# One plain half of the up projection instead of two: product 2 summed in PSUM onto a copy of product 1, and the rows of hn made on two engines

## The chip, the cores and the metric

The kernel runs on one core of one Trainium2 chip. The metric is the device time of one execution in microseconds (us); lower is better.

## What is computed

One encoder layer on 512 tokens of width 2048, all in float32. The change lies in the second half of the layer:

```python
h = rms_norm(x, pre_ffn_g)                        # 512 x 2048
up = causal_dwconv(h @ w_up, conv_w, conv_b)      # w_up is 2048 x 11264
y = (gelu(up[..., :5632]) * up[..., 5632:]) @ w_down
x = x + rms_norm(y, post_ffn_g)
```

`causal_dwconv` is a three-tap convolution along the tokens, channel by channel. Ahead of it stand the attention, the pooling and the projection with `w_o`, which the change does not touch.

## The kernel before

**Numbers.** Every matmul operand is split into a rounded high part (ScalarE, line 140) and a low rest (VectorE, line 141). A plain product is three matmuls of 512 columns: high by high, high by low, low by high (`mm3`, lines 162, 164 and 165).

**Units and halves.** The up projection is cut into 22 units `u` with two halves each: `p = 0` goes through the gelu (`gate`), `p = 1` is multiplied onto it (`product`). A half is 256 channels. Channels lie on the partitions and the 512 tokens along the free axis.

**Two ways to compute a half.** The first `PLAIN` halves are plain: 16 blocks of 128 rows of the contraction, by 2 blocks of channels, by 3 matmuls, 96 matmuls in all. Every other half `k` uses seven products of 2 by 2 blocks in place of eight (channel blocks, halves of the contraction, halves of the tokens), numbered 1 to 7. One product (`mm2`) is 8 wide matmuls (line 170: the high part of the weight factor by the high and low parts of the token factor side by side, 512 columns) and 8 narrow ones (line 176: the low part of the weight factor by the high part of the token factor, 256 columns). Products in `TURNED` (4, 6 and 7) issue the narrow ones first.

**Factors.** The token factors are made once. `turn_back` transposes the normalized rows `hn` on TensorE (line 1012), ScalarE scales them out of PSUM (line 1017) into whole blocks, and they are split into `hT` (printed as `gT`), which serve products 1, 2, 4 and 7. `h_sums` then forms the sums for products 5, 6 and 3 on VectorE (lines 1381 to 1387) and splits them (tiles `h5`, `h6`, `h3`); it also turns the block for product 7 into a difference, which is split back into `hT`. The weight factors are made on the fly. `Factors.load` brings a block of `w_up` from HBM, `make` splits it into `wfh` and `wfl`, and then an adding DMA of GpSimd (`add`, line 1110) puts another block on top of the raw tile, which makes the next factor that shares it. For product 7 of a half the tile is the one of product 3 (`wy`): split for 3, then added to, then split for 7. There are four pairs of `wfh` and `wfl`.

**Banks.** Products 1, 6, 7 and 4 of a half accumulate in one PSUM bank `qa`; ScalarE copies the sum out after 6 and after 7 (lines 1421 and 1427). Products 5 and 3 use `qg` (3 uses `qe` in the first four halves), product 2 uses `qd`. After product 1, ScalarE copies one half of `qa` and VectorE adds the other half (lines 1406 and 1407); after product 2, VectorE adds both halves of `qd` (lines 1410 and 1411).

**Order.** The order of the products on TensorE is a table (`Factors.order`): first products 1 and 2 of halves 0 to 3, while `hn` is still being made for tokens 256 to 511; then the plain halves, between which the transposes are placed by hand; then products 5, 3, 6, 7 and 4 of the halves 0 to 3; then all seven products of each later half, interleaved with the half before, at places 7 apart. TensorE runs in the order in which the code is written. On the other engines a scheduler fixes the order when the program is built. Each of these engines works through its queue in that order. `sums_in_dram` (`more_sums`) issues copies and adding DMAs of 1 MB blocks of `w_down` beside this; one step is issued after each quarter of a plain half.

Of the kernel before, what the change touches and what calls it, by code (L numbers as in the profile page):

```python
# [15 lines left out]
P = 128  # L16
# [11 lines left out]
EPS = 1e-6  # L28
WARM = 9
NU = KF // 2  # L30
PLAIN = 2
CU = 4
AHEAD = 3
SCALE = 1.0 / math.sqrt(DH)
# [47 lines left out]
def encoder_layer(ctx: ExitStack, tc: tile.TileContext, x, xT, vecs, rel, post_mix, post_ffn,  # L82
# [23 lines left out]
    def bank(name):  # L106
        return psum.tile([P, 512], F32, tag="ps", name=name)
# [107 lines left out]
    def part(w, *idx):  # L215
        return tuple(v[(slice(None),) + idx] for v in w)
# [685 lines left out]
    if True:  # L902
# [100 lines left out]
        def quarter(k, t, i):  # L1003

            return tuple(hT[2 * k + i][:, :, at, :] for at in AT[t])

        def turn_back(t0, pair, ps):

            for k in range(2):
                kb = 2 * pair + k  # L1010
                for t in range(2):
                    nc.tensor.transpose(ps[:, k * T + t * P:k * T + (t + 1) * P],
                                        hn[t0 + t][:, kb * P:(kb + 1) * P], ident)
            v = wholes[pair // 4, t0 // 2]
            for k in range(2):
                kb = 2 * pair + k
                nc.scalar.activation(v[:, kb % 8, :], ps[:, k * T:(k + 1) * T], AF.Copy, scale=col(V_PREFFN, kb))
            if pair % 2:
                i = pair // 2 % 2
                split(*quarter(pair // 4, t0 // 2, i), v[:, 4 * i:4 * i + 4, :])  # L1020
# [43 lines left out]
        class Factors:  # L1064
# [3 lines left out]
            def __init__(self):  # L1068
                n = 2 * NU - PLAIN

                self.alone, self.open = (1, 2, 3, n - 1), False
                place_of = {1: 0, 6: 8, 2: 2, 7: 10, 5: 4, 4: 12, 3: 6}
                begin = [(k, i) for k in range(4) for i in (1, 2)]
                lone = {5: 0, 3: 2, 6: 4, 7: 6, 4: 8}
                end = [(n - 1, 5), (n - 2, 6), (n - 1, 3), (n - 1, 1), (n - 2, 7), (n - 1, 6), (n - 2, 4),
                       (n - 1, 7), (n - 1, 2), (n - 1, 4)]
                order = sorted([(5 * k + at, k, i) for k in range(4) for i, at in lone.items()] +
                               [(18.5 + 7 * (k - 4) + at, k, i) for k in range(4, n) for i, at in place_of.items()])  # L1080
                self.order = begin + [(k, i) for _, k, i in order if (k, i) not in begin + end] + end
                self.order[8:8] = [("w", q) for q in range(4 * PLAIN)]
                self.raw, self.made, self.loaded, self.used = {}, [], 0, 0
# [75 lines left out]
            hn[t] = acc8(f"hn{t}", "A")  # L1159
        for l in range(2):  # L1160
            cs = slice(l * D // 2, (l + 1) * D // 2)
            for t in range(2, 4):
                nc.vector.tensor_scalar_mul(hn[t][:, cs], xn[t][:, cs], rn[:, t:t + 1])
        for k in range(2):
            wholes[k, 1] = whole_tile(h8(2 + k, f"a2{k + 1}"))

# [139 lines left out]
    if True:  # L1306
# [67 lines left out]
        def h_sums():  # L1374
            def keep(n, i, at, v):
                hs.setdefault(n, {})[i] = h8(at, f"h{n}{i}", F32R).rearrange("p (a b c) -> p a b c", a=4, b=2)
                split(*(hs[n][i][:, :, p, :] for p in range(2)), v)

            halves = [[wholes[k, t][:, 4 * i:4 * i + 4, :] for k in range(2) for t in range(2)] for i in range(2)]
            for i, (a11, a21, a12, a22) in enumerate(halves):  # L1380
                nc.vector.tensor_sub(a22, a22, a21)
                keep(5, i, (1, 0)[i], a22)
                nc.vector.tensor_sub(a21, a11, a21)
                nc.vector.scalar_tensor_tensor(a22, a22, -1.0, a11, op0=ALU.mult, op1=ALU.subtract)
                keep(6, i, (4, 5)[i], a22)
            for a11, a21, a12, a22 in halves:
                nc.vector.scalar_tensor_tensor(a12, a22, -1.0, a12, op0=ALU.mult, op1=ALU.subtract)
            for i in range(2):
                keep(3, i, (3, 2)[i], halves[i][2])
            return [v[1] for v in halves]  # L1390

        banks, gates = {}, {}

# [8 lines left out]
        def keep(k, i):  # L1402

            if i == 1:
                v = zs[k, "1"] = first_parts[:, k % 4, :]
                nc.scalar.activation(v, banks[k, "a"][:, :T], AF.Copy)
                nc.vector.tensor_add(v, banks[k, "a"][:, T:], v)
            elif i == 2:
                v, d = zs[k, "1"], banks.pop((k, "d"))
                nc.vector.tensor_add(v, d[:, :T], v)  # L1410
                nc.vector.tensor_add(v, d[:, T:], v)
            elif i in (5, 3) and k < 4:
                return
            elif i == 5:
                zs[k, "5"] = raw_x("zb")[:, :S] if k == end else holder("m8")[1]
                nc.scalar.activation(zs[k, "5"], banks[k, "g"], AF.Copy)  # L1416
            elif i == 6:
                m = raw_x("zm") if k == end else holder("m8")[2]
                zs[k, "m"] = m.rearrange("p (a b c) -> p a b c", a=2, b=2)
                v = wide(zs[k, "m"][:, :1])  # L1420
                keep.copied = nc.scalar.activation(v, banks[k, "a"], AF.Copy).ins
                nc.vector.tensor_add(v, banks[k, "g"] if k < 4 else banks.pop((k, "g")), v)
                if k < 4:
                    nc.vector.tensor_add(v, banks.pop((k, "e")), v)
            elif i == 7:
                v = wide(zs[k, "m"][:, 1:])
                nc.scalar.activation(v, banks[k, "a"], AF.Copy)
                nc.vector.tensor_add(v, banks.pop((k, "g")) if k < 4 else zs.pop((k, "5")), v)
            elif i == 4:
                keep_all(k)  # L1430

        def keep_all(k):
            one, m, a = zs.pop((k, "1")), zs.pop((k, "m")), banks.pop((k, "a"))
            z = new_z()
            nc.scalar.activation(z[:, 0, :T], one, AF.Copy)
            nc.vector.tensor_add(z[:, 1].rearrange("p (a b) -> p a b", a=2), m[:, :, 0], m[:, :, 1])
            nc.scalar.activation(z[:, 0, T:], a[:, T:], AF.Copy)
            nc.vector.tensor_add(z[:, 0, T:], a[:, :T], z[:, 0, T:])
            u, p = divmod(PLAIN + k, 2)
            if p:  # L1440
                product(u, gates.pop(u), z)
            elif k == 2:
                zs["late"] = u, z
            else:
                gates[u] = gate(u, z)

        def seven(k, i):
            w = factors.get()
            at = "e" if i == 3 and k < 4 else BANK[i]
            fresh = i in FIRST or at == "e"  # L1450
            if fresh:
                banks[k, at] = bank(f"q{at}_{k}")
            mm2(banks[k, at], w, [h_factor(i, kb) for kb in range(8)], fresh, i in TURNED)
# [25 lines left out]
        turn(2, 3)  # L1479
        behind_h.append((split.last, split.rest))  # L1480
        factors.open = True
        def plain(p, behind):
            ups = [bank(f"up{p}_{j}") for j in range(2)]
            for q in range(4):
                factors.used += 1
                factors.prefetch(0)
                with ExitStack() as behind_split:
                    for ins in behind_h[q] if not p and q < 2 else ():
                        behind_split.enter_context(tc.issue_after(ins))
                    factors.prefetch(factors.AHEAD if p else (1, 2, 3, factors.AHEAD)[q])  # L1490
                w = weights.get(f"w{p}0_{q}", 0)
                for kb in range(4 * q, 4 * q + 4):
                    for j in range(2):
                        mm3(ups[j], part(w, j, slice(kb % 4 * P, (kb % 4 + 1) * P)), g_both(hT, kb),
                            kb == 0, kb == KD - 1)
                behind(q)
            return ups

        def turn_two(q):
            if q < 2:  # L1500
                turn(4 + 2 * q, 5 + 2 * q)

        def keep_a21(q):
            more_sums(1)
            if q < 2:
                split(*quarter(0, 1, q), a21_11[q])

        ups = plain(0, turn_two)
        a21_11 = h_sums()
        gates[0] = gate(0, plain_z(ups))  # L1510
        ups = plain(1, keep_a21)
        product(0, gates.pop(0), plain_z(ups))
        rights, firsts = [right(0, cc) for cc in range(2)], []
        for r in rights:
            next(r)
# [6 lines left out]
        for k, i in factors.order[8 + 4 * PLAIN:]:  # L1522
            seven(k, i)
            keep(k, i)
            if (k, i) == (3, 6):
                u, z = zs.pop("late")
                with tc.issue_after(keep.copied):
                    gates[u] = gate(u, z)
# [260 lines left out]
```

## Time and profile before

| | |
|---|---|
| median of 3 runs | 1849.39 us (1848.6 to 1849.62) |
| profiled execution | 1850.36 us, of which the span of the trace is 1848.6 us |
| TensorE busy | 1838.0 us, 99% of the span |
| VectorE, ScalarE, GpSimd busy | 1483.9, 1099.8 and 306.6 us |
| the two plain halves and the transposes between them | 572.8 to 618.4 us |

The span is the time from the first to the last instruction of the trace. In a timeline row the first number is the start, the second the duration in us; rows that follow each other with the same form are merged and counted (x8). Square brackets give the idle time of the engine just before, and what ended it. PE is TensorE, PEld its weight loads, DVE VectorE, ACT ScalarE, POOL GpSimd, SP SyncE; SPq and POOLq are DMA queues.

### The profile page before, as it was taken

To read this page: it belongs to the slowest core of one execution; us is meant where nothing else is said; L and a number is where in the kernel's file an instruction comes from. 1 tells how busy PE (TensorE), PEld (TensorE's weight loads), DVE (VectorE), ACT (ScalarE), POOL (GpSimd) and SP (SyncE) were. 2 spreads that over 40 slices of the span, in tenths; PEclk is the share of its full clock that TensorE was granted. 3 is DMA by queue.
4 is the path that set the end of the run, shared out by engine and by line. 5 is a ranking of instruction groups with operands and counts; after the bars stand their busy time and mean duration, and the time that the engine had idled before them with its cause. 6 is when DMAs were issued, how large, how long until landed. Compare 5 with 4: busy or idle time off the path is not lost.

```text
span 1848.6 us, 25317 instructions
## 1 busy us (share of the span) xinstructions
PE 1838.0 (99%) x9514; PEld 1578.3 (85%) x9514; DVE 1483.9 (80%) x1776; ACT 1099.8 (59%) x1438; POOL 306.6 (17%) x407
## 2 busy tenths in 40 slices
PE   9999999999999999999999999999999999999998
PEld 7888888888888888888888888888888888888886
DVE  6988778878678787777777777777777899899876
ACT  7655555457586666665656666666655655555553
POOL 3411000100001222122122222221221011111101
PEclk9999999999999999999999999999999999999999
DMA  8599978999979988988889899898888977777785
GB/s 319 170 320 301 320 228 235 276 262 318 337 270 291 214 198 208 208 199 200 207 205 198 203 201 204 196 209 201 204 176 302 360 222 162 193 215 176 177 230 158
DMA packets 139546, 428.63 MB, mean 232 GB/s; under 512 B 12000, under 2 KB 15456, under 8 KB 133728
## 3 DMA queue, kind: packets, MB, share of 16 engines
q0 software_dynamic: 55440, 175.66, 47.0%
q1 hardware_dynamic: 83984, 251.36, 38.5%
q8 instruction: 75, 1.23, 0.3%
q14 instruction: 47, 0.39, 0.1%
HBM read 372.97 MB, written 104.33 MB: 258 GB/s over the span
## 4 chain that ended last, share of the span: by engine, by line
PE 98%; DMA 1%; DVE 0%; SPq 0%; issue 0%; ACT 0%; DVEq 0%; POOLq 0%; POOL 0%; ACTq 0%
PE qa L170 19%; PE qa L176 10%; PE qg L170 9%; PE qg L176 5%; PE qd L170 5%; PE pa L164 4%; PE pa L165 4%; PE pa L162 4%; PE m L165 3%; PE m L164 3%; PE m L162 3%; PE qd L176 2%; PE pg L164 2%; PE pg L165 2%; PE pg L162 2%; PE v L164 2%
## 5 line engine op out<-in xcount | busy, mean ns | idle before, releaser
L170 PE MATMUL qa<-gT,wfh 128*128 128x512 f32 x1176 | 294.4, 392 | 0.0
L141 DVE TENSOR_TENSOR wfl<-x,wfh 128x1024 fp32r<-128x1024 f32 x161 | 197.0, 1224 | 83.0 <-ACT wfh L140 80.8
L170 PEld LDWEIGHTS qa<-gT,wfh 128*128 128x128 f32 x1176 | 211.6, 189 | 37.9
L140 ACT ACTIVATE wfh<-x 128x1024 fp32r<-128x1024 f32 x161 | 170.1, 1057 | 92.4 <-PE qg L170 46.2
L1110 POOL DMA_DIRECT2D x<-in_w_up x122 | 104.6, 858 | 460.8 <-DVE wfl L141 429.2
L176 PE MATMUL qa<-gT,wfl 128*128 128x256 f32 x1176 | 164.5, 283 | 0.0
L170 PE MATMUL qg<-h,wfh 128*128 128x512 f32 x640 | 158.2, 389 | 0.6 <-ACT m L1416 0.6
L176 PEld LDWEIGHTS qa<-gT,wfl 128*128 128x128 f32 x1176 | 154.8, 191 | 4.1
L170 PEld LDWEIGHTS qg<-h,wfh 128*128 128x128 f32 x640 | 120.0, 188 | 25.9 <-ACT m L1416 1.0
L141 DVE TENSOR_TENSOR bl<-b,bh 128x2048 fp32r<-128x2048 f32 x56 | 127.1, 2286 | 18.4 <-ACT bh L140 11.7
L140 ACT ACTIVATE wfh<-wy 128x1024 fp32r<-128x1024 f32 x98 | 103.3, 1054 | 63.7 <-PE qd L170 49.6
L140 ACT ACTIVATE bh<-b 128x2048 fp32r<-128x2048 f32 x56 | 106.0, 1912 | 55.5 <-DVE b L1230 23.0
L141 DVE TENSOR_TENSOR wfl<-wy,wfh 128x1024 fp32r<-128x1024 f32 x98 | 119.4, 1218 | 10.2 <-ACT wfh L140 7.9
L162 PE MATMUL pa<-bh,ah 128*128 128x512 f32 x320 | 124.5, 389 | 0.0
L164 PE MATMUL pa<-bl,ah 128*128 128x512 f32 x320 | 124.5, 389 | 0.0
L165 PE MATMUL pa<-bh,al 128*128 128x512 f32 x320 | 124.5, 389 | 0.0
L170 PE MATMUL qd<-gT,wfh 128*128 128x512 f32 x392 | 97.0, 390 | 0.0
L176 PEld LDWEIGHTS qg<-h,wfl 128*128 128x128 f32 x640 | 87.3, 190 | 6.2
L176 PE MATMUL qg<-h,wfl 128*128 128x256 f32 x640 | 89.2, 282 | 0.0
L170 PEld LDWEIGHTS qd<-gT,wfh 128*128 128x128 f32 x392 | 73.3, 188 | 15.0
L170 PE MATMUL qa<-h,wfh 128*128 128x512 f32 x336 | 84.1, 392 | 0.0
L141 DVE TENSOR_TENSOR wfl<-wz,wfh 128x1024 fp32r<-128x1024 f32 x49 | 59.9, 1222 | 28.5 <-PE qa L170 25.4
(574 smaller groups left out, 4335.9 us busy)
## 6 DMA issues: line engine op xcount, KB each, us to landing
x<-in_w_up POOLq DMA_DIRECT2D x122, 512.0 KB, 6.5
b<-in_w_down SPq DMA_DIRECT2D x32, 1024.0 KB, 6.8
wt<-in_w_o POOLq DMA_DIRECT2D x24, 1024.0 KB, 15.5
wz<-in_w_up SPq DMA_DIRECT2D x42, 512.0 KB, 6.0
x<-in_w_up SPq DMA_DIRECT2D x42, 512.0 KB, 5.1
wy<-in_w_up SPq DMA_DIRECT2D x42, 512.0 KB, 4.2
wy<-in_w_up POOLq DMA_DIRECT2D x42, 512.0 KB, 6.6
sum<-part POOLq DMA_DIRECT2D x38, 512.0 KB, 6.9
```

Source lines behind the costliest of these rows:

```text
L140: rounded = nc.scalar.activation(hi, src, AF.Copy)
L141: rest = nc.vector.tensor_sub(lo, src, f32(hi))
L162: nc.tensor.matmul(ps, l[0], r[0], start=first, stop=False, skip_group_check=onto)
L164: nc.tensor.matmul(low, l[0], r[1], start=False, stop=False, skip_group_check=onto)
L165: nc.tensor.matmul(ps, l[1], r[0], start=False, stop=last, skip_group_check=onto)
L170: nc.tensor.matmul(ps, w[0][:, kb], pairs[kb][0], start=fresh and not kb, stop=last, skip_group_check=not fresh)
L176: nc.tensor.matmul(ps[:, sl], w[1][:, kb], pair[:, sl], start=False, stop=last, skip_group_check=not fresh)
L1110: nc.gpsimd.dma_start(self.raw[k, what], self.block(k, m, kh), accum_op=ALU.add)
```

## The change

There is now one plain half, and the half that was plain is computed in seven products, as half `k = 0` of 43 where there were 42. What else is written differently:

```diff
-PLAIN = 2
+PLAIN = 1
...
-                    nc.tensor.transpose(ps[:, k * T + t * P:k * T + (t + 1) * P],
-                                        hn[t0 + t][:, kb * P:(kb + 1) * P], ident)
+                    nc.tensor.matmul(ps[:, k * T + t * P:k * T + (t + 1) * P], hn[t0 + t][:, kb * P:(kb + 1) * P],
+                                     ident, start=not k and not t, stop=True, is_transpose=True,
+                                     skip_group_check=True)
...
-                begin = [(k, i) for k in range(4) for i in (1, 2)]
+                begin = [(0, 1), (1, 1), (0, 2), (2, 1), (1, 2), (3, 1), (2, 2), (3, 2)]
...
-                order = sorted([(5 * k + at, k, i) for k in range(4) for i, at in lone.items()] +
+                order = sorted([(1 if (k, i) == (1, 5) else 5 * k + at, k, i) for k in range(4) for i, at in lone.items()] +
...
-            for t in range(2, 4):
-                nc.vector.tensor_scalar_mul(hn[t][:, cs], xn[t][:, cs], rn[:, t:t + 1])
+            nc.scalar.activation(hn[2][:, cs], xn[2][:, cs], AF.Copy, scale=rn[:, 2:3])
+            nc.vector.tensor_scalar_mul(hn[3][:, cs], xn[3][:, cs], rn[:, 3:4])
...
             if i == 1:
-                v = zs[k, "1"] = first_parts[:, k % 4, :]
-                nc.scalar.activation(v, banks[k, "a"][:, :T], AF.Copy)
-                nc.vector.tensor_add(v, banks[k, "a"][:, T:], v)
+                banks[k, "d"] = bank(f"qd_{k}")
+                keep.copied = nc.scalar.activation(banks[k, "d"], banks[k, "a"], AF.Copy).ins
             elif i == 2:
-                v, d = zs[k, "1"], banks.pop((k, "d"))
-                nc.vector.tensor_add(v, d[:, :T], v)
+                v, d = first_parts[:, k % 4, :], banks.pop((k, "d"))
+                zs[k, "1"] = v
+                nc.scalar.activation(v, d[:, :T], AF.Copy)
                 nc.vector.tensor_add(v, d[:, T:], v)
...
-            fresh = i in FIRST or at == "e"
+            fresh = i in (1, 5) or at == "e"
...
-        ups = plain(0, turn_two)
-        a21_11 = h_sums()
+        turn(4, 5)
+        ups = [bank(f"up0_{j}") for j in range(2)]
+        for q in range(4):
...
+            more_sums(1)
+            if not q:
+                turn(6, 7)
+            if q == 1:
+                h_sums()
         gates[0] = gate(0, plain_z(ups))
-        ups = plain(1, keep_a21)
-        product(0, gates.pop(0), plain_z(ups))
...
-            if (k, i) == (3, 6):
+            if (k, i) in ((2, 7), (5, 1)):
```

So product 2 no longer starts its bank afresh: it adds onto a ScalarE copy of product 1 and waits for that copy. The transposes of pairs 4 and 5 stand ahead of the plain half instead of after its first quarter. `h_sums` is written after the second quarter of the only plain half instead of after the first of two; the split of the difference for product 7 is now inside it. Row block 2 of `hn` is made by ScalarE, row block 3 by VectorE.

On VectorE, this is the stretch that leads up to the low part of the weight factor of product 3 of half 0 (`wfl` from `wy`). In the kernel before:

```order
L141 TENSOR_TENSOR h61_5671<-a22_5257,h61_5671 128x4x256
L1311 SCALAR_TENSOR_TENSOR zc_5682<-zc_5682,vec_69 128x511 x2
L141 TENSOR_TENSOR h30_5676<-a12_5003,h30_5676 128x4x256
L1312 SCALAR_TENSOR_TENSOR zc_5682<-zc_5682,vec_69 128x510 x2
L141 TENSOR_TENSOR wfl_5695<-wx_5150,wfh_5694 128x1024
L141 TENSOR_TENSOR gT0_4822<-a21_5256,gT0_4822 128x4x256
L141 TENSOR_TENSOR wfl_5727<-wy_5537,wfh_5726 128x1024
```

In the changed kernel:

```order
L141 TENSOR_TENSOR h61_5597<-a22_5257,h61_5597 128x4x256
L141 TENSOR_TENSOR gT0_4822<-a21_5256,gT0_4822 128x4x256
L141 TENSOR_TENSOR gT1_4823<-a21_5256,gT1_4823 128x4x256
L141 TENSOR_TENSOR h30_5606<-a12_5003,h30_5606 128x4x256
L141 TENSOR_TENSOR wfl_5618<-x01_5497,wfh_5617 128x1024
L141 TENSOR_TENSOR h31_5609<-a12_5003,h31_5609 128x4x256
L141 TENSOR_TENSOR wfl_5650<-wy_5500,wfh_5649 128x1024
L141 TENSOR_TENSOR wfl_5655<-wx_5150,wfh_5654 128x1024
```

The low part of product 3's factor stands in both behind nearly all of `h_sums`; from the first row of `h_sums` (line 1382) to it there are 20 VectorE instructions in the changed kernel.

On ScalarE, this is the stretch that holds the high part of the factor of product 7 of half 0 and the copy of `qa` after product 6. In the kernel before (`wfh_5835` is the factor):

```order
L1310 ACTIVATE m8_5822<-zc_5682,vec_69 128x512
L140 ACTIVATE wfh_5835<-wy_5537 128x1024
L1435 ACTIVATE zc_5682<-first_parts_5274 128x256
L140 ACTIVATE wfh_5856<-wy_5622 128x1024
L1310 ACTIVATE m8_5822<-zc_5682,vec_69 128x512
L140 ACTIVATE wfh_5878<-wx_5150 128x1024
L1421 ACTIVATE m8_5822<-qa_0_5275 128x512
```

In the changed kernel (`wfh_5696` is the factor):

```order
L140 ACTIVATE wfh_5649<-wy_5500 128x1024
L140 ACTIVATE wfh_5654<-wx_5150 128x1024
L1437 ACTIVATE zc_5684<-first_parts_5274 128x256
L140 ACTIVATE wfh_5696<-wy_5500 128x1024
L1334 ACT_TABLE_LOAD
L1334 ACTIVATE zc_5684<-zc_5684 128x1024
L140 ACTIVATE wfh_5717<-wy_5547 128x1024
L1423 ACTIVATE m8_5784<-qa_0_5275 128x512
```

The table load and the gelu of unit 0 now stand between this factor and the copy of `qa`; in the kernel before they stand nine rows ahead of this factor.

More of the change, by code (lines that the diff above doesn't have):

```diff
@@ L1385, in h_sums @@
                 keep(6, i, (4, 5)[i], a22)
-            for a11, a21, a12, a22 in halves:
+            for i, (a11, a21, a12, a22) in enumerate(halves):
                 nc.vector.scalar_tensor_tensor(a12, a22, -1.0, a12, op0=ALU.mult, op1=ALU.subtract)
             for i in range(2):
+                split(*quarter(0, 1, i), halves[i][1])
+            for i in range(2):
                 keep(3, i, (3, 2)[i], halves[i][2])
-            return [v[1] for v in halves]
         banks, gates = {}, {}
@@ L1426, in keep @@
                 v = wide(zs[k, "m"][:, 1:])
-                nc.scalar.activation(v, banks[k, "a"], AF.Copy)
+                keep.copied = nc.scalar.activation(v, banks[k, "a"], AF.Copy).ins
                 nc.vector.tensor_add(v, banks.pop((k, "g")) if k < 4 else zs.pop((k, "5")), v)
@@ L1441, in keep_all @@
                 product(u, gates.pop(u), z)
-            elif k == 2:
+            elif k in (1, 3):
                 zs["late"] = u, z
@@ L1481, in encoder_layer @@
         factors.open = True
[L1482 to L1503, printed above, removed]
+        turn(4, 5)
+        ups = [bank(f"up0_{j}") for j in range(2)]
+        for q in range(4):
+            factors.used += 1
+            factors.prefetch(0)
+            with ExitStack() as behind_split:
+                for ins in behind_h[q] if q < 2 else ():
+                    behind_split.enter_context(tc.issue_after(ins))
+                factors.prefetch((1, 2, 3, factors.AHEAD)[q])
+            w = weights.get(f"w00_{q}", 0)
+            for kb in range(4 * q, 4 * q + 4):
+                for j in range(2):
+                    mm3(ups[j], part(w, j, slice(kb % 4 * P, (kb % 4 + 1) * P)), g_both(hT, kb),
+                        kb == 0, kb == KD - 1)
             more_sums(1)
-            if q < 2:
-                split(*quarter(0, 1, q), a21_11[q])
-        ups = plain(0, turn_two)
-        a21_11 = h_sums()
+            if not q:
+                turn(6, 7)
+            if q == 1:
+                h_sums()
         gates[0] = gate(0, plain_z(ups))
-        ups = plain(1, keep_a21)
-        product(0, gates.pop(0), plain_z(ups))
         rights, firsts = [right(0, cc) for cc in range(2)], []
```

## The prediction

> **What bounds the kernel now.** I read the page first: busy time by engine, and the chain that ended last.
>
> ```profile
> PE 1838.0 (99%) x9514; PEld 1578.3 (85%) x9514; DVE 1483.9 (80%) x1776; ACT 1099.8 (59%) x1438; POOL 306.6 (17%) x407
> PE 98%; DMA 1%; DVE 0%; SPq 0%; issue 0%; ACT 0%; DVEq 0%; POOLq 0%; POOL 0%; ACTq 0%
> ```
>
> TensorE is the chain. Then the waits of TensorE over the whole trace, of which this is the longest that is not at the program's start:
>
> ```profile
> PE qg L170 <- ACT m L1416: 0.6, 1, 0.6
> ```
>
> So only TensorE's own work can be saved, any new wait of TensorE costs its full length, and what VectorE saves is worth nothing by itself. Third, TensorE's timeline around the plain halves: start of the second plain half, start of the seven-product part (0,5), start of product (0,7), and a later product, ten products after (0,5).
>
> ```profile
> 596.57 0.39 PE L162 MATMUL up<-gT,w_0h 128*128 128x512 f32 x1
> ...
> 618.33 1.98 PE L170 MATMUL qg<-h,wfh 128*128 128x512 f32 x8
> ...
> 629.46 1.12 PE L176 MATMUL qa<-gT,wfl 128*128 128x256 f32 x8
> ...
> 646.19 1.98 PE L170 MATMUL qe<-h,wfh 128*128 128x512 f32 x8
> ```
>
> **The change part by part.** I write (k,i) for product i of half k.
>
> *One plain half becomes seven products.* The plain half takes 618.33 - 596.57 = 21.76 us. Ten products take 646.19 - 618.33 = 27.86, one 2.786, seven 19.50. Gain 2.26 us, all of it on the chain.
>
> *Product 2 onto the copy.* Per half, ScalarE copies 512 columns instead of 256 and later 256 more; VectorE loses two adds. Both engines have room (59 and 80%). What counts is whether product 2 waits for the copy. In the steady part:
>
> ```profile
> 1212.38 2.00 PE L170 MATMUL qa<-gT,wfh 128*128 128x512 f32 x8
> ...
> 1215.17 1.12 PE L176 MATMUL qa<-h,wfl 128*128 128x256 f32 x8
> ...
> 1217.97 1.98 PE L170 MATMUL qd<-gT,wfh 128*128 128x512 f32 x8
> 1215.86 0.37 ACT L1406 ACTIVATE first_parts<-qa 128x256 f32<-128x256 f32 x1
> ...
> 1218.17 0.60 ACT L1421 ACTIVATE m<-qa 128x512 f32<-128x512 f32 x1 [0.68 <-PE qa L170]
> ```
>
> Product 1 ends at 1215.17, product 2 begins one product later, at 1217.97, and ScalarE gets to product 1's bank at 1215.86. With the 0.60 us of a copy of 512 columns it would be done at 1216.46, 1.5 us early. The copy after product 6 already has the same distance to product 7 and holds up nothing. I cost this at nothing; if ScalarE came more than 1.5 us later than now, the cover would be gone, in up to 39 halves.
>
> *hn on two engines.* Now:
>
> ```profile
> 564.17 2.74 DVE L1163 TENSOR_SCALAR hn<-x,small 128x1024 f32<-128x1024 f32 x4 [0.81 <-POOL small L999]
> ...
> 568.82 1.57 ACT L1017 ACTIVATE a<-xt,vec 128x256 f32<-128x256 f32 x4
> ...
> 578.44 1.03 PE L1012 MATMUL xt<-ident,hn 128*128 128x128 f32 x8
> ```
>
> Two halves of a row block on ScalarE take about 2.0 us (1.06 us each for 128x1024, rows below) and end near 566.2, before the first group of transposes behind it is read, at 568.82. Nothing. The transposes of pairs 4 and 5 now follow directly on 2 and 3: TensorE makes a group in 1.03 us, ScalarE reads one in 1.57. With all eight banks in use the second group can wait for a read: between 0 and 1.6 us; I take the difference of the two, 0.5. Their number stays the same; the new form of the transposes costs nothing.
>
> *The cover for h_sums and for the first factors.* Here is the price. Two plain halves hid the work of VectorE; now one does. VectorE's stretch before, first and last of 16 rows, then the low part of the factor of (0,3), GpSimd's adding DMA that makes the factor of (0,7):
>
> ```profile
> 583.31 1.23 DVE L1381 TENSOR_TENSOR a<-a,a 128x1024 f32<-128x1024 f32 x1
> ...
> 600.77 1.22 DVE L141 TENSOR_TENSOR h<-a,h 128x1024 fp32r<-128x1024 f32 x1
> ...
> 609.18 1.23 DVE L141 TENSOR_TENSOR wfl<-wy,wfh 128x1024 fp32r<-128x1024 f32 x1 [1.15 <-ACT wfh L140]
> 610.71 0.86 POOL L1110 DMA_DIRECT2D wy<-in_w_up x1 [2.62 <-DVE wfl L141]
> DMA to landing us min/median/max: 5.2/7.0/8.5
> ```
>
> The 16 rows stand 17.46/15 = 1.16 us apart. In the changed order 20 such instructions reach from the first of h_sums to the low part of (0,3). The first can start when pair 5 is transposed, scaled and split. Before, that was 583.31, 4.9 us after its transposes (578.44). Now the transposes come some 5.5 us earlier, but ScalarE and VectorE have the pairs 2 and 3 and the splits of the plain weights in front of it: bounds 577.6 and 583.3, I take 580.8, the middle rounded up for that queue. The low part ends at 580.8 + 20 x 1.16 = 604.0. GpSimd starts 0.3 us later (610.41 to 610.71), the data land 7.0 us on (median; 5.2 to 8.5): 611.3. Adding DMAs of 1 MB blocks share that queue and now stand ahead of it, so I do not take the minimum.
>
> TensorE arrives at (0,7) after the plain half and four products: 596.57 + 0.5 + 4 x 2.786 = 608.2. Before, GpSimd's add began at 610.71 and TensorE came at 629.46, 18.7 us later; now the add begins at 604.3 and TensorE comes 3.9 us later, so the factor's high part can start only at 611.3. And (0,7) also needs the copy of qa after (0,6), which stands in ScalarE's queue behind this factor, the table load, the gelu and another factor:
>
> ```profile
> 605.85 1.28 ACT L1333 ACT_TABLE_LOAD   x1 [0.87 <-DVE zc L1312]
> 607.14 1.06 ACT L1333 ACTIVATE zc<-zc 128x1024 f32<-128x1024 f32 x1
> 608.11 1.04 ACT L140 ACTIVATE wfh<-wy 128x1024 fp32r<-128x1024 f32 x1
> 609.06 1.04 ACT L140 ACTIVATE gT<-a 128x1024 fp32r<-128x1024 f32 x1
> ```
>
> From start to start that is 0.95 + 1.29 + 0.97 + 0.95, plus the copy's 0.60: 4.8 us. TensorE goes on at 611.3 + 4.8 = 616.1. The wait is 7.9 us. Bounds: start 577.6 and landing 5.2 give 2.9; start 583.3 and landing 8.5 give 11.9. What is late next is (1,7), whose DMA starts once (1,3) is split, right behind the copy; it has four products (11 us) of cover and I cost it at nothing.
>
> *The clock.* An idle TensorE loses its clock. The window with its last matmuls, the one behind it, then the program's start:
>
> ```profile
> 1840.00:1842.00 2.00, 0.35 (x3) 0.14 (x2) 1.32 (x5) 0.51 (x2) 0.25 (x1) 1.00 0.00 0
> 1842.00:1844.00 2.00, 0.00 (x0) 0.00 (x0) 1.67 (x3) 0.00 (x0) 0.29 (x1) 0.70 0.02 8
> 1.09 4.21 PE L133 MATMUL idle<-early 128*128 128x128 f32 x18 [1.09 <-DVE mhalf L129]
> 4.96 0.77 PE L162 MATMUL q<-gT,q_0h 128*128 128x512 f32 x1
> ...
> 6.48 0.39 PE L162 MATMUL k<-gT,k_0h 128*128 128x512 f32 x1
> ```
>
> The granted clock (third number from the right) falls from 1.00 within some 2.5 us of the last matmul, and at the start a matmul takes 0.77 us until TensorE has worked for 5.4 us (1.09 to 6.48), then 0.39. So a wait of 7.9 us is followed by some 5.4 us at half speed, which loses 2.7; between 0 (no drop) and 2.7.
>
> The Trainium skill, in "TensorE: Matmul & The Clock Gate", Part 1, has it that the clock is halved after an idle window of about 3.4 us and given back after a busy window of the same length. By that figure the loss would be 1.7 and the sum below 1 us smaller.
>
> *The rest.* The later gates, the DMA steps issued earlier and the additional factor's seven transfers (against four) have as cover the products beside them; more than 2 us of waiting in a steady half would have to come up before TensorE saw it.
>
> *Sum*, against the profiled execution: 1850.36 - 2.26 + 0.5 + 7.9 + 2.7 = 1859.2. The profiled execution lies 0.97 above the median of the runs, so 1858.2 beside the median; I say 1858.
>
> **The rivals.**
>
> *The block for (0,7) lands under cover (not slower).* If the add landed by 608.2 - 4.8 = 603.4, nothing would wait and only the saving would be left: 1849.39 - 2.26 + 0.5 = 1847.6. For that the low part of (0,3) would have to be ready at 596, eight us before my count, some seven VectorE instructions. For it speaks that TensorE saw no such wait before; against it the fixed order and the 1.16 us per instruction, which leave 2.9 us of wait even at the lower bounds. A partial cover is in my range.
>
> *Product 2 waits for its copy all along.* If ScalarE reached the copies late, each half would wait: 0.5 us in each of 39 halves is 19.5 us on top of my sum, 1877. For it: ScalarE's queue also waits for DMAs. Against it: the 1.5 us above, and the copy after product 6, which has the same distance.
>
> *TensorE waits, but the clock stays.* 1858.2 - 2.7 = 1855.5. It needs the wait to fall short of the drop, and the end of the trace speaks against that.
>
> **How the numbers follow.** The wait at (0,7) has 0.82, of which 0.12 is the case in which the clock stays; cover 0.13; waits for the copies 0.05. The likeliest gives 1858. Its own range is 1852 (wait of 2.9, clock loss 1.7) to 1862 (wait of 11.9). The range 1850.5 to 1863 takes in these bounds and leaves out nearly all of the cover and copy cases, 0.18. About 0.2%, 3.7 us, is what a measurement of this kernel can tell from no change. The saving of 2.26 is below that, so the cover case counts as the same, apart from 0.03 for a gain I have not seen. Slower: 0.78 of the wait case and the copy case, 0.83. Same: 0.14.
>
> **What would show it.** In the trace after: a single idle time of TensorE of 6 to 10 us ahead of the narrow matmuls of (0,7), some 36 us after its first transposes of hn, ended by VectorE's wfl or by ScalarE's copy of qa; ScalarE waiting for the landing of wy just ahead of it; matmuls of twice the length and a granted clock under 1 right behind it; no waits between product 1 and 2 later on; seven products in 19.5 us. I would be wrong if VectorE got to (0,3) much earlier, or if waits for copies came up in every half.

## The result and the profile after

The changed kernel takes 1864.46 us (median of 6 runs, 1861.37 to 1866.97) against 1849.57 us of the kernel before on the same chip: 1.0079 of it, 95% interval 1.0066 to 1.0092. In a second series of 5 runs it took 1862.36 us against 1850.42, 1.0065 (1.0053 to 1.0078). It is slower, as forecast; the forecast of 1858.0 was too low, and the first median lies 1.5 us above the upper end of the range, 1863.0. The profiled execution took 1861.37 us, 11.0 more than the profiled one of before; it was the fastest of its six. One run of e9 below, 2567 us at a mean granted clock of 0.67, is left out of its numbers.

TensorE's busy time is the same (1838.1 and 1838.0 us) although it has less to do: what the plain half saves comes back as slower matmuls, which stand further down. The rest of the loss is in its waits. The two lines of the page, then TensorE's waits (total, times, longest):

```profile
PE 1838.1 (99%) x9530; PEld 1579.1 (85%) x9530; DVE 1463.8 (79%) x1698; ACT 1128.1 (61%) x1490; POOL 310.0 (17%) x411
...
PE 95%; DVE 2%; DMA 2%; ACT 1%; issue 1%; SPq 0%; POOL 0%; DVEq 0%; POOLq 0%; ACTq 0%
```

```profile
PE qa L176 <- ACT m L1423: 9.8, 1, 9.8
...
PE qg L170 <- ACT m L1418: 1.0, 2, 0.9
...
PE xt L1012 <- ACT a L1018: 0.2, 1, 0.2
```

Before, the chain that ended last was TensorE for 98%; now VectorE, a DMA and ScalarE are in it with 5%, where a DMA had 1%. There is one new long wait, 9.8 us. TensorE's timeline shows the place: start of the plain half, of (0,5), the wide matmuls of (0,6), then (0,7), and the product behind it.

```profile
573.52 0.50 PE L162 MATMUL up<-gT,w_0h 128*128 128x512 f32 x1
...
596.33 1.98 PE L170 MATMUL qg<-h,wfh 128*128 128x512 f32 x8
...
605.65 2.00 PE L170 MATMUL qa<-h,wfh 128*128 128x512 f32 x8
617.45 2.08 PE L176 MATMUL qa<-gT,wfl 128*128 128x256 f32 x8 [9.80 <-ACT m L1423]
619.33 2.88 PE L170 MATMUL qa<-gT,wfh 128*128 128x512 f32 x8
622.05 1.98 PE L170 MATMUL qe<-h,wfh 128*128 128x512 f32 x8
```

The wait stands ahead of the narrow matmuls of (0,7). Behind it the same eight narrow matmuls take 2.08 us instead of 1.12: half clock. The chain of waits through this stretch, in order of time, tells what TensorE waited for (start, length, what):

```profile
580.27 1.22 DVE a L1382
...
601.85 1.22 DVE wfl L141
603.07 0.29 issue
603.36 9.10 DMA wy<-in_w_up
...
612.69 0.92 issue
613.62 1.28 ACT L1334
...
615.13 0.74 issue
615.87 1.04 ACT wfh L140
616.91 0.49 ACT m L1423
617.45 2.08 PE qa L176 x8
```

From top to bottom: `h_sums` and the splits on VectorE up to the low part of (0,3); GpSimd's adding DMA for (0,7), 9.1 us; then ScalarE's queue, in which the split of the new factor, the table load, the gelu and another split stand ahead of the copy of `qa`. Of that split and of the gelu, 1.06 us each, this view counts most as issue. ScalarE's row for the split shows that it had sat idle until the add landed:

```profile
612.54 1.06 ACT L140 ACTIVATE wfh<-wy 128x1024 fp32r<-128x1024 f32 x1 [5.91 <-DMA wy<-in_w_up]
```

Last, the granted clock (third number from the right) in five windows of 3.41 us that begin where TensorE ran dry:

```profile
607.60:611.01 3.41, 0.05 (x1) 0.00 (x0) 0.00 (x0) 0.00 (x0) 0.86 (x1) 1.00 1.04 270
611.01:614.42 3.41, 0.00 (x0) 0.00 (x0) 0.79 (x1) 1.86 (x2) 0.00 (x0) 0.50 1.08 219
614.42:617.83 3.41, 0.38 (x2) 0.38 (x2) 1.32 (x2) 3.40 (x5) 0.00 (x0) 0.50 1.01 241
617.83:621.24 3.41, 3.41 (x13) 3.02 (x13) 3.41 (x5) 2.51 (x3) 0.86 (x1) 0.50 0.51 103
621.24:624.65 3.41, 3.41 (x19) 2.93 (x19) 2.71 (x4) 1.19 (x2) 1.68 (x2) 1.00 0.94 208
```

TensorE works from 617.45 to 621.24 at half clock and so loses 3.79 / 2 = 1.9 us. The number beside the clock is the share of the DMA engines: they are full (1.04 and 1.08) while TensorE waits.

### The profile page after: what moved, and what is told of

It is laid out like the page before. It is cut to its first block, busy times and chain, and to the rows that moved or that the text cites. A ratio compares the mean times of both kernels' runs of the same rounds, so it can differ in the third digit from the quotient of the medians.

```text
span 1859.6 us, 25316 instructions
## 1 busy us (share of the span) xinstructions
PE 1838.1 (99%) x9530; PEld 1579.1 (85%) x9530; DVE 1463.8 (79%) x1698; ACT 1128.1 (61%) x1490; POOL 310.0 (17%) x411
## 4 chain that ended last, share of the span: by engine, by line
PE 95%; DVE 2%; DMA 2%; ACT 1%; issue 1%; SPq 0%; POOL 0%; DVEq 0%; POOLq 0%; ACTq 0%
PE qa L170 19%; PE qa L176 10%; PE qg L170 9%; PE qd L170 5%; PE qg L176 5%; PE pa L162 4%; PE pa L165 4%; PE pa L164 4%; PE m L162 3%; PE m L164 3%; PE m L165 3%; PE qd L176 2%; PE pg L162 2%; PE pg L165 2%; PE pg L164 2%; PE u L164 2%
## 5 line engine op out<-in xcount | busy, mean ns | idle before, releaser
L170 PE MATMUL qa<-gT,wfh 128*128 128x512 f32 x1200 | 301.3, 393 | 0.0
L141 DVE TENSOR_TENSOR wfl<-x,wfh 128x1024 fp32r<-128x1024 f32 x165 | 202.1, 1225 | 92.9 <-ACT wfh L140 74.1
L170 PEld LDWEIGHTS qa<-gT,wfh 128*128 128x128 f32 x1200 | 216.7, 189 | 38.9
L140 ACT ACTIVATE wfh<-x 128x1024 fp32r<-128x1024 f32 x165 | 174.4, 1057 | 80.0 <-PE qg L170 49.8
L176 PE MATMUL qa<-gT,wfl 128*128 128x256 f32 x1200 | 168.8, 284 | 9.8 <-ACT m L1423 9.8
L176 PEld LDWEIGHTS qa<-gT,wfl 128*128 128x128 f32 x1200 | 158.7, 192 | 14.4 <-ACT m L1423 10.2
L170 PE MATMUL qg<-h,wfh 128*128 128x512 f32 x656 | 162.5, 390 | 1.1 <-ACT m L1418 1.0
```

The lines of the kernel that those rows point to most:

```text
L140: rounded = nc.scalar.activation(hi, src, AF.Copy)
L141: rest = nc.vector.tensor_sub(lo, src, f32(hi))
L170: nc.tensor.matmul(ps, w[0][:, kb], pairs[kb][0], start=fresh and not kb, stop=last, skip_group_check=not fresh)
L176: nc.tensor.matmul(ps[:, sl], w[1][:, kb], pair[:, sl], start=False, stop=last, skip_group_check=not fresh)
```

## The experiments

All are timed against the kernel before on the same chip. For e1 to e4 its median was 1849.66 us, for e5 to e8 1850.42, for e9 and e10 1850.39, for e11 1849.76.

### e1: everything but the plain half

```diff
 # the kernel before, PLAIN = 2, with
+                banks[k, "d"] = bank(f"qd_{k}")
+                keep.copied = nc.scalar.activation(banks[k, "d"], banks[k, "a"], AF.Copy).ins
 ...
+            nc.scalar.activation(hn[2][:, cs], xn[2][:, cs], AF.Copy, scale=rn[:, 2:3])
+            nc.vector.tensor_scalar_mul(hn[3][:, cs], xn[3][:, cs], rn[:, 3:4])
```

> The kernel before with everything of the change except the plain half: product 2 on the ScalarE copy, hn on two engines, the new form of the transposes, the new order of the first eight products. Theory (the loss sits at product (0,7) alone, the rest costs nothing): 1849.5 us, within 1 us, and no wait of TensorE over 0.6 us behind the program's start. Rival (the copies cost something in the steady halves; that is the part of the loss which the profiled run does not show, 1864.5 - 1861.4 = 3.1 us): 1852 to 1853, with waits at product 2.

Measured: 1851.37 us (1849.28 to 1852.59, 11 runs), 1.0006 of before (0.9997 to 1.0015). TensorE's largest group of waits behind the program's start (total, times, longest):

```profile
PE qg L170 <- ACT m L1417: 1.2, 2, 0.8
```

No product 2 waits for its copy. The waits for a copy of `qg` are 0.6 us more than before (1.2 against 0.6); the interval holds no change and ends at 0.15%, 2.8 us. The median is 0.9 us above what the theory allowed and one wait of 0.8 us above its 0.6, but neither is at product 2, where the rival had put them. So these parts cost 2.8 us at most, and the rest of the loss belongs to the plain half and to what moved with it (the places of the transposes, of `h_sums` and of (1,5), which this run leaves as they were).

### e2: more work inside the wait

```diff
-            mm2(banks[k, at], w, [h_factor(i, kb) for kb in range(8)], fresh, i in TURNED)
+            for _ in range(4 if (k, i) == (0, 3) else 1):
+                mm2(banks[k, at], w, [h_factor(i, kb) for kb in range(8)], fresh, i in TURNED)
```

> The changed kernel with product (0,3) computed four times in a row into its fresh bank: 3 x 2.8 = 8.4 us more of matmuls just ahead of the place of the wait. Theory (TensorE has 9.8 us to spare there, and the idle time costs a further 1.8 us of clock): the work disappears in the wait, about 1.4 us of it are left, the clock stays at 1.00, and the kernel gets 1.8 us faster, 1862.7. Rival A (TensorE's own queue is the bound): 8.4 us slower, 1872.9. Rival B (the clock has nothing to do with the idle time): same time, 1864.5, with matmuls of double length still there.

Measured: 1864.75 us (1863.69 to 1868.05), 1.0083 (1.0070 to 1.0096). From the start of (0,5) to that of (1,3) the profile has 28.3 us against 25.7 in the changed kernel, 2.6 more, where rival A asks for 8.4. TensorE's timeline, (0,7) and the product behind:

```profile
622.25 1.83 PE L176 MATMUL qa<-gT,wfl 128*128 128x256 f32 x8 [4.12 <-DVE wfl L141]
623.88 2.99 PE L170 MATMUL qa<-gT,wfh 128*128 128x512 f32 x8
626.70 2.01 PE L170 MATMUL qe<-h,wfh 128*128 128x512 f32 x8
```

TensorE really had room here; rival A falls. The expected 1.8 us did not come, for two reasons. 4.1 us of wait were left and not 1.4, because the scheduler now placed the copy of `qa` behind two more splits on ScalarE (1.9 us) and the add took 9.9 us (0.8 more). (The row names a split on VectorE, which ended 0.02 us after that copy.) And these 4.1 us were enough for the clock: (0,7) took 4.45 us (622.25 to 626.70) in place of 2.8. What was measured, the time and the double length, is what rival B said, so this run does not decide about the clock. In e8 and e11 below it stays where the waits are short.

### e3: product 7 two places later

```diff
+                late = {(1, 5): 1, (0, 7): 9.2, (0, 4): 11.2}
-                order = sorted([(1 if (k, i) == (1, 5) else 5 * k + at, k, i) ...
+                order = sorted([(late.get((k, i), 5 * k + at), k, i) ...
```

In this kernel the sums of halves 0 and 1 after product 6 share a tile, so half 0's channels come out wrong; the work and its order stay.

> The changed kernel with (0,7) two products later on TensorE, behind (1,3) and (1,6), and (0,4) behind it. Theory (only the cover is missing): 2 x 2.8 = 5.6 us more of cover, the copy after (0,6) no longer last; a wait of 1 to 3 us is left, no loss of clock: 1850 to 1852. Rival (the wait moves to (1,3), (1,6) or (1,7), whose factors stand in the same queues): 1856 to 1860, with a wait of 5 us or more at one of these.

Measured: 1859.5 us (1857.83 to 1862.33), 1.0054 (1.0041 to 1.0067). No wait is left at (0,7), but there are waits of 1.92 us at (0,6), 1.73 at (1,7) and 2.52 at (2,7), and the clock fell to half twice, in (0,6) and in (2,7). The 9.8 us became 6.2, and none of them where the theory put them: the rival was right that the wait moves and on the time, but of its places only (1,7) came, and no single wait reached its 5 us. At (1,7) the copy of `qa` stood again behind a split for which ScalarE had sat 5.65 us until the add landed. (0,6) stands ahead of the product that was moved; there ScalarE had sat 2.94 us for an add that landed 15.1 us after its issue, behind a transfer of 1 MB. (The profiled run, 1862.28, also had 2.2 us of waits far ahead of the change, in the attention and the pooling.)

### e4: other loads out of the add's way

```diff
+                elif i == 5 and k in (2, 3):          # the same for (4, 1)
+                    self.raw[k, "x"] = raw_x("wx")
+                    self.put_off.append(k)
...
+            def load_put_off(self):
+                for n in self.put_off:
+                    with tc.issue_after(self.last):
+                        self.last = nc.gpsimd.dma_start(self.raw[n, "x"], self.block(n, 0, 0)).ins
...
+                    last = self.add(k, "x", 0, 1)     # for k = 0 the add for (0,4)
+                    if not k:
+                        self.last = last.ins
+                        self.load_put_off()
```

The comments are not in the code.

> The changed kernel with the loads of the first factors of (2,5), (3,5) and (4,1) taken off SyncE's queue, where two of them start 1.4 us ahead of the adding DMA for (0,7), and issued on GpSimd behind the adds for (0,7) and (0,4). Theory (the add took 9.1 us to land, against 5.2 before, because five transfers of 512 KB share the DMA engines): it lands in 6 to 7.5 us, the wait falls from 9.8 to 7 to 8, the time by 2 to 3 us to about 1862. Rival (an adding DMA in this place takes that long by itself): landing of 9 us, 1864.5.

Measured: 1861.59 us (1860.43 to 1864.12), 1.0064 (1.0052 to 1.0077). The add for (0,7) from issue to landing (the last number, 9.1 us in the changed kernel's view of its DMA issues), and TensorE's row at (0,7):

```profile
wy<-in_w_up POOLq DMA_DIRECT2D x1, 512.0 KB, 6.3
```

```profile
615.13 2.08 PE L176 MATMUL qa<-gT,wfl 128*128 128x256 f32 x8 [6.96 <-ACT m L1445]
```

The landing falls by 2.8 us and the wait by the same 2.8, from 9.8 to 7.0. So these 2.8 of the 9.1 us come from the transfers beside the add, and are not its own time. 1.0 us of it came back as a wait at (1,7). The time alone does not show the gain: the ratio is that of the changed kernel's second series (1.0065).

### e5: the changed kernel again

> The changed kernel once more, for a second profile. Theory: the wait at (0,7) is again 9 to 10.5 us, set by an add that lands in 9 to 10 us and by the copy of qa behind it, and costs 1.6 to 2.7 us of clock on top; what else differs between runs lies ahead of the up projection, in stages that the change does not touch (the plain half started at 575.6 and 577.1 in two of the runs above, at 573.5 in the first profile). Rival: the 3.1 us between the first profile and the median lie in the steady halves, as waits of product 2 for its copy.

Measured: 1862.36 us (1860.31 to 1863.65). The wait at (0,7) was again 9.80 us, the add landed in 9.1 us, the clock loss was 1.4 us (619.09 to 621.97 at half clock), no product 2 waited. The plain half began at 575.16 and not 573.52; of these 1.6 us, 1.0 is a wait in the pooling. So the wait and the landing repeat to 0.1 us, and the difference between the two profiles lies ahead of the change. Why the runs of the changed kernel spread over 3 to 6 us within such a series, and those of before over 2 to 6, no profile shows in full.

### e6: the factor of (0,3) ahead of h_sums

```diff
             if q == 1:
+                factors.prefetch(3)
+                factors.make(0, 3)
+                factors.before[0, 3] = factors.made.pop()
                 h_sums()
```

> The changed kernel with the weight factor of (0,3) split ahead of h_sums on VectorE, so that the adding DMA for (0,7) starts at about 588 instead of 603 and has landed long before TensorE comes. Theory (the wait is the chain VectorE - add - ScalarE's queue): the add is off the chain and what is left is ScalarE's order, the copy of qa behind the factor of (1,3), the table load, the gelu and the factor of (0,4): a wait of about 4 us at (0,7) instead of 9.8, about 1 us at (1,5), whose split is now later; 1858 to 1861. Rival (the add was not the bound, ScalarE's queue alone makes the wait): 9 to 10 us as before, 1864.5.

Measured: 1860.34 us (1859.54 to 1861.03, 4 runs), 1.0054 (1.0041 to 1.0068). GpSimd's row of the add for (0,7), then ScalarE's rows up to the copy of `qa`, then TensorE at (0,7):

```profile
588.98 0.86 POOL L1112 DMA_DIRECT2D wy<-in_w_up  x1 [1.86 <-DVE wfl L141]
```

```profile
605.01 1.06 ACT L140 ACTIVATE wfh<-wy 128x1024 fp32r<-128x1024 f32 x1 [2.94 <-DMA wy<-in_w_up]
...
607.98 1.28 ACT L1338 ACT_TABLE_LOAD   x1
609.28 1.06 ACT L1338 ACTIVATE zc<-zc 128x1024 f32<-128x1024 f32 x1
615.12 1.06 ACT L140 ACTIVATE wfh<-wx 128x1024 fp32r<-128x1024 f32 x1 [4.78 <-DMA wx<-in_w_up]
616.08 0.58 ACT L1427 ACTIVATE m<-qa 128x512 f32<-128x512 f32 x1
```

```profile
616.71 2.07 PE L176 MATMUL qa<-gT,wfl 128*128 128x256 f32 x8 [7.55 <-ACT m L1427]
```

The add starts 14 us earlier and lands 16.0 us on, behind a transfer of 1 MB; its factor is split at 605.01, ahead of TensorE's arrival at 609.16. The wait falls by 2.3 us only: the copy of `qa`, ready to run from 609.2 on, stands behind the factor of (0,4), and ScalarE sits there for 4.78 us until that factor's own add lands, after 10.2 us. The theory was right on the time, on the 1.0 us at (1,5) and on what is left at (0,7) (ScalarE's order), and short by 3.5 us on its size: it had no wait for that add.

### e7 and e8: the copy first, and the sums for product 3 last

```diff
+            SHORT = 15, 16                     # how far splits run ahead: the one for (0,4) comes later
...
+                self.prefetch(2 if self.used in self.SHORT else self.AHEAD if self.open else min(self.AHEAD - 1, 9 - self.used))
...
+            with tc.issue_after(keep.copied) if (k, i) == (0, 7) else nullcontext():
+                seven(k, i)
...
+            if (k, i) == (0, 7):
+                with tc.issue_after(keep.copied):
+                    nc.scalar.activation(flat(gates[0]), flat(gates[0]), AF.Gelu_apprx_tanh)
 # e8 also:
+            if q == 2:
+                rest()                         # the splits for product 3, out of h_sums
```

The comments are not in the code; both kernels also have the edit of e6.

> As the kernel before this one in the list, and on ScalarE the copy of qa after (0,6) ahead of the factor of (0,4), the table load and the gelu of unit 0 behind the copy after (0,7). Theory: with both taken off the chain about 1 us is left at (1,5), 1 us at (0,7), little at (1,7), and the clock stays at 1.00: 1850 to 1854, the same as before. Rival (the wait moves to (0,4), whose own add starts at 604.5 and took 10.5 us to land): 3 us or more there, 1855 to 1859.

> As the kernel before this one in the list, and the split of the sums for product 3 written behind the third quarter of the plain half, so that the factor of (1,5) is split ahead of it on VectorE. Theory: the 1 us at (1,5) falls to 0.5 or less, about 0.6 us stay at (0,7), about 1.5 us at (1,7): 1849 to 1853. Rival (the sums for product 3 come late for (0,3) now, over 1 us of wait there): 1852 to 1856.

Measured: e7 1856.37 us (1854.77 to 1859.32), 1.0035 (1.0023 to 1.0048); e8 1857.3 us (1855.0 to 1859.21), 1.0038 (1.0024 to 1.0052). TensorE's timeline at (0,7) and (0,4) in e8:

```profile
608.91 1.22 PE L176 MATMUL qa<-gT,wfl 128*128 128x256 f32 x8 [0.69 <-ACT m L1431]
...
617.14 1.99 PE L176 MATMUL qa<-gT,wfl 128*128 128x256 f32 x8 [2.41 <-ACT m L1437]
```

At (0,7) 0.7 us are left in both, as expected, and 0.69 us do not touch the clock. The rival of e7 came as well: the wait has moved to (0,4), 2.53 us in e7 and 2.41 in e8, with 1.7 us of clock behind it; the add for (0,4) took 9.8 and 9.7 us to land. In e8 the 1.0 us at (1,5) is gone and 1.2 us stand at (1,7), as expected; its rival's wait at (0,3) did not come, and the time is above the ranges of both and no better than e7's. Of the 11.9 us that the changed kernel loses in this series (e5), about half is gone.

### e9 and e10: still fewer transfers beside the add for (0,4)

These are e8 with the edit of e4, for (3,5) alone and for all three loads.

> The kernel of the last run before (split of (0,3) first, copy first, sums for product 3 last) with one load more moved: the first block for (3,5), needed only 12 products later, is issued on GpSimd behind the add for (0,4). Theory (the wait of 2.4 us that is left at (0,4), and the 1.7 us of clock behind it, come from an add that shares the DMA engines with four other transfers): the add lands 1.5 to 2.5 us earlier, the wait falls under 1.5 us, the clock stays at 1.00, about 1 us stays at (1,7): 1852 to 1854. Rival (the next add in the row, for (1,7), is pushed back instead): same time as the kernel it starts from, 1856 to 1858, with the wait at (1,7).

> As the kernel before this one in the list, with the first blocks for (2,5) and (4,1) moved too. Theory: the add for (0,4) lands in about 7.5 us as in the run that moved these three loads alone, no wait at (0,4); but (2,5) and (1,7) have less cover, up to 2 us at (1,7): 1851 to 1855. Rival (the loads come late for (2,5)): a wait of 2 us or more there, 1856 or above.

Measured: e9 1859.85 us (1859.36 to 1866.48, 5 runs, of which two lie 5 us and more above the other three), 1.0066 (1.0052 to 1.0079); e10 1861.48 us (1860.51 to 1864.37), 1.0063 (1.0051 to 1.0075). The waits at (1,7), first e9, then e10:

```profile
629.78 2.08 PE L176 MATMUL qa<-gT,wfl 128*128 128x256 f32 x8 [3.96 <-ACT m L1448]
```

```profile
633.95 2.08 PE L176 MATMUL qa<-gT,wfl 128*128 128x256 f32 x8 [5.39 <-ACT m L1453]
```

Both rivals came true in the waits; the time of e9 is 2 us above its rival's range. The wait at (0,4) is gone, and 4.0 and 5.4 us stand at (1,7), 2.8 more in e10 at (2,5). At (2,5) it is the load put off that is late, with its add. At (1,7) the copy of `qa` stands behind a split on ScalarE, which had sat for the add to another factor (4.86 us in e9, 2.67 in e10).

### e11: three loads left out

```diff
+                    if (k, i) in ((2, 5), (3, 5), (4, 1)):
+                        nc.gpsimd.memset(tile_, 0.0)
+                    else:
                         nc.sync.dma_start(tile_, self.block(k, m, kh))
```

> The kernel with split of (0,3) first, copy first and the sums for product 3 last (median 1857.3), with the 512 KB loads of the first blocks of (2,5), (3,5) and (4,1) left out: GpSimd fills these tiles with zeros, so these three factors lack their first block. Theory (what is left of the loss is the DMA engines, 100% busy in this stretch, which move the wait from one add to the next): the add for (0,4) lands in 6 to 7.5 us instead of 9.7, the waits at (0,4) and behind it fall to about 1 us in all, the clock stays at 1.00: 1851 to 1853. Rival (the chain of split, add and split by itself takes too long, whatever the transfers beside it): a wait of 2 us or more stays at (0,4) or (1,7), 1855 to 1858.

Measured: 1856.05 us (1851.85 to 1862.28, 9 runs), 1.0039 (1.0026 to 1.0053). In the profiled run (1854.3) the add for (0,4) landed in 5.2 us, against 9.7 in e8, the wait at (0,4) was gone, and the clock never left 1.00 in this stretch. What remained was 0.73 us at (0,3), 0.69 at (0,7) and, the longest, this at (1,7):

```profile
627.10 1.22 PE L176 MATMUL qa<-gT,wfl 128*128 128x256 f32 x8 [1.65 <-ACT m L1434]
```

So for the place and the clock the theory holds: with 1.5 MB less in this stretch the add is quick. For the rest neither side holds in full: 3.1 us of waits are left and not 1, no wait reaches the 2 us of the rival, and against the kernel before the ratio is that of e8 (1.0039 and 1.0038), in the rival's range. At (1,7) the copy of `qa` stands once more behind a split that had waited for its add, 0.90 us; what ScalarE's order alone would cost there is not shown. That its nine runs spread over 10 us, beside 3 us for the kernel before on the same chip, is not explained; the profile is of a run below the median.

No version beat the kernel before.

## Why the prediction was right and wrong

**The one plain half.** Up to the start of (0,5) the changed kernel gains 21.32 us from the start of (0,1) on ((0,1) at 548.65 and 547.97, (0,5) at 618.33 and 596.33), and pays seven products of 2.786 for it: -1.82. The prediction had -2.26 for the half and +0.5 for the transposes, -1.76. The sum is right. Of the 0.44 us between -2.26 and -1.82 the wait for a bank is 0.16; for the other 0.28 no wait stands in the trace.

**Product 2 on the copy, hn on two engines.** Costed at nothing; e1 bounds them at 0.15%, 2.8 us, and no product 2 waits in e1 or e5.

**The wait at (0,7).** Right in place, in cause and in each link but one: VectorE's stretch began at 580.27 (forecast 580.8), ended at 603.07 (604.0), the add began at 603.36 (604.3), TensorE arrived at 607.65 (608.2), ScalarE's queue took 4.9 us (4.8). The step that failed is the landing. I took the median of the old kernel's adds, 7.0 us, with 8.5 as the upper bound; it was 9.1, 9.1 and 9.9 in three profiles (e2 the third). The wait became 9.8 us and not 7.9. I had asked what is queued ahead of the add, and not what runs beside it: the step that packs the work on TensorE packs the issues too. In the changed kernel five transfers of 512 KB are issued within 3.2 us (601.32 to 604.49); before, the neighbours of this add stood 3.5 us ahead and 3.2 us behind. e4 shows the price: with the two loads of these five issued behind it the landing is 6.3.

**The clock.** Right that it falls, too high in size: 1.9 and 1.4 us, not 2.7. I had taken the 5.4 us from the program's start. The rule of the Trainium skill that stood beside it ("TensorE: Matmul & The Clock Gate", Part 1), by which one busy window of about 3.4 us gives the clock back, would have given 1.7, an estimate from that page. The trace agrees: 617.83 to 621.24 is the first window in which TensorE is busy throughout, and the clock is back at its end. With the other half of the rule, an idle window ahead of the fall, the traces do not agree: in e3 the clock fell behind a window that was busy for 1.48 of 3.40 us.

**(1,7), at no cost.** Right in the changed kernel, where the delay at (0,7) gave (1,7) its cover. It holds no longer once (0,7) is mended: e3, e4 and e8 to e11 all show a wait there, of 1.0 to 5.4 us.

**The sum.** Against the profiled run: 1859.2 forecast, 1861.37 measured. The wait is 1.9 over, the clock 0.8 under; the remaining 1.1 is 0.4 more of `qg` waits, 0.6 behind TensorE's last matmul, 0.8 that no single wait shows behind (0,5), less 0.7 that the run was ahead at (0,1). Then came a step that I did not cost: I carried the profile's 0.97 above the median over to the changed kernel. Its profiled run was the fastest of six, 3.1 us below the median. That, more than the landing, put the median outside the range; in the second series it lies inside. Part of the spread lies ahead of the change ((0,1) began between 547.97 and 551.51 in the profiles of e2 to e11 and of the changed kernel), part is the phase of the clock (a loss of 1.4 us in e5, 1.9 in the changed kernel's first profile); the rest stays open.

**The rivals.** The cover case fell by 9.8 us. Waits in every half: none (e1, e5). TensorE waits and the clock stays: not at 9.8 us, nor at 2.4 (e8), but at 1.73 in e3 and 2.78 in e10.

## What to carry to other kernels

Work that is cut from the busiest engine is also cover: before the cut, list what the other engines do in its shadow, and follow that queue to the first result that is needed on the other side. Count the transfers that the shorter stretch will issue together: a landing time read from the loose schedule can be too short for the tight one (7.0 us taken, 9.1 measured). And once a chain of equal steps has no slack, a mend at one place moves the wait to the next (from (0,7) to (0,4) to (1,7)); even with three loads left out, 3.1 us of waits remained.

## What the hardware showed

The clock moves on windows of its own, not on the length of the wait. In every run that lost it, it stayed at half for 3.4, 6.8 or 10.2 us: 10.2 in the changed kernel (611.0 to 621.2) and in e4 and e5, 6.8 in e6, e9 and e10, 3.4 in e2, e7, e8 and, twice, in e3. The two falls in e3 stand 37.55 us apart (610.87 and 648.42), 11 times 3.41. In e3 a wait of 1.92 us cost the clock and one of 1.73 us did not. Its windows, placed on the fall at 610.9 (TensorE's busy time is the number after the length, the clock the third from the right):

```profile
607.50:610.90 3.40, 1.48 (x13) 1.28 (x12) 1.87 (x3) 2.00 (x2) 0.61 (x2) 1.00 0.98 243
610.90:614.30 3.40, 3.40 (x13) 2.82 (x11) 3.40 (x6) 2.01 (x3) 1.37 (x2) 0.50 1.05 274
614.30:617.70 3.40, 3.40 (x21) 2.99 (x20) 0.87 (x1) 2.30 (x3) 1.72 (x2) 1.00 1.06 222
...
624.50:627.90 3.40, 1.67 (x12) 1.39 (x11) 1.56 (x2) 2.66 (x4) 0.00 (x0) 1.00 1.07 255
627.90:631.30 3.40, 3.40 (x22) 3.06 (x23) 3.40 (x5) 2.63 (x4) 0.57 (x1) 1.00 1.02 271
```

The window in which TensorE was busy for 1.48 of 3.40 us was followed by one at half clock, the one with 1.67 was not. A window need not be idle throughout, then. In e10 even a wait of 2.78 us left the clock at 1.00: it lay across two windows (621.18 to 624.59 and on to 628.01, as counted from the fall at 631.42), in which TensorE was busy for 1.51 and 2.53 us. So the limit lies here near 1.5 of 3.4 us. On the way back, a window at half clock that was busy for 2.50 of 3.41 us did not return the clock (e9), one with 2.88 did (e5). The clock can fall after TensorE has gone on (e2: resumed at 622.25, fell at 622.6), and a wait of 2 us cost up to 1.7 us more (e3).
